# A decoder layer on one core: y's first two quads turned once for both token blocks, and diff queries and keys copied two units earlier

## The chip, the core and the metric

The kernel runs on one core of a Trainium2 chip. The metric is the device time of one execution in microseconds (us). The engines are named as in the profile: PE is TensorE (PEld its weight loads), DVE is VectorE, ACT is ScalarE, POOL is GpSimd and SP is SyncE. SP and POOL issue the transfers (DMA). Each engine takes its instructions in the order in which they stand in its queue, and an instruction that waits holds back all those behind it.

## The reference

One decoder layer in float32 for 256 tokens of width 2048: a half-step SwiGLU feed-forward net, a token mixer, a second feed-forward net, each followed by a residual sum and a layer norm. The change lies in the mixer, which is, cut to what matters:

```python
c_q, c_kv, k_r, dq, dk, dv, gate_mla, gate_diff = _split_columns(h @ w_in)
o_mla  = _mla_attention(q, k, v_mla)            # 8 heads, from c_q, c_kv, k_r
o_diff = _diff_attention(dq, dk, dv, positions, lam)   # 4 heads, two maps each
y = jax.nn.sigmoid(gate_mla) * (o_mla @ w_br_mla) + jax.nn.sigmoid(gate_diff) * (o_diff @ w_br_diff)
return y @ w_out
```

Here `dq`, `dk` and `dv` are 256 x 1024 each, and `y` is 256 x 2048.

## The kernel before, in words

**Tiles and units.** The 256 tokens are two blocks of 128 (b = 0 and 1). A product takes activations with the contracted dimension on the partitions as PE's stationary operand and a strip of weights as the moving one, and leaves a bank of 128 tokens x 512 columns. To keep float32 accuracy every operand is split into a high and a low part (`split`, L153-L156: a cast on ACT, L154, and a subtraction on DVE, L155), and each product is done three times (`triple`, L208-L210). Weights come from memory as 512 KB tiles `raw` or `sraw` (through SP in the main), are split into a pair of tiles of the ring `wring`, and are used. One such tile is a *unit* of work: 12 products when it serves both token blocks, 6 in the products of the seven-product scheme (`Hybrid`).

**Order of the work.** The program is written as a stream of units (`unit`, `advance`): load, split, and some units later the products. After the products of every unit a clock `tick` runs; `later(n, fn)` puts a piece of work n ticks ahead. So the rest of the layer (turning, softmax, norms) is threaded between the products by due times counted in units. A planner then places each engine's instructions: it goes by this order among those whose data it reckons to be there, and may put a later one first. In the last part of the mixer (`project`) each unit's products for block 1 come after the next unit's products for block 0, so block 1 of a result is done one unit after block 0.

**Turning a result.** A result has tokens on the partitions; the next product needs its columns there. Some results are turned on PE (`rows_to_quad`, L668 on; the transpositions are L671). Others make a trip through memory: `turn_out` (L711-L718) turns 32 x 32 blocks on DVE (`blocks`, L715) and writes them with four transfers on POOL (L717, 64 KB each) to a `turn` tensor in memory, arranged so that a plain read gives the whole turned; `turn` (L723-L731) reads it back `wait` units later with one POOL transfer into a tile `turned` (L729, 256 KB), and hands it to its user `more` units after that. The user is either a put into an activation quad (a quad is 512 columns, split by L154 and L155) or an ACT copy (L737, `turn_to_cols`) into a tile of columns.

**Where it happens.** `pair_cols` makes the turned diff queries and keys, `dqT` and `dkT`, four trips each (two halves, two blocks), with the copy 10 units after the read. `branch_diff` and `branch_mla` make y in four quads f = 0..3: first the four `branch_diff` results (4 units each), then the four `branch_mla` results (4 units each), and in its `done` (L1374-L1376 on DVE) the sum with the two gates; the sum lies in the tile that the profile calls `diff`. Quads 0 and 1 of y go through memory, quads 2 and 3 over PE. The product with `w_out` follows at once and takes the quads in order, two units a quad; its first products need quad 0. The layer norm after it, created just before, fetches rows through SP into tiles of the tag "tmp".

**Slots.** Tiles share slots by tag: "tmp" has 6 slots of 128 x 512 (the trips' `blocks` and `turned`, results before turning, rows for the norm), "act" has 41 of 128 x 1024. A tile waits for a slot until an earlier one's last reader is done.

Of the kernel before, what the change touches and what calls it, by code (L numbers as in the profile page):

```python
# [11 lines left out]
F32 = mybir.dt.float32  # L12
# [6 lines left out]
P = 128  # L19
# [40 lines left out]
def layer_kernel(ctx: ExitStack, tc: tile.TileContext, a: dict, out: bass.AP):  # L60
    nc = tc.nc
    V, S, GP, PE = nc.vector, nc.scalar, nc.gpsimd, nc.tensor
# [9 lines left out]
    def nm(s):  # L72
        uid[0] += 1
        return f"{s}_{uid[0]}"

    def act_tile(shape, dt=F32, name="act"):
        return apool.tile(shape, dt, tag="act", name=nm(name), bufs=SLOTS)

    def tmp_tile(shape, name="tmp", dt=F32):
        return small.tile(shape, dt, tag="tmp", name=nm(name), bufs=6)  # L80
# [22 lines left out]
    def later(n, fn):  # L103
        uid[0] += 1
        heapq.heappush(todo, (step[0] + n, uid[0], fn))
# [562 lines left out]
    def rows_to_quad(src, b, x, q, gain=None, shift=None, shared=False):  # L668
        t = tr_bank()
        for i in range(4):  # L670
            PE.transpose(t[:, i * P:(i + 1) * P], src[:, i * P:(i + 1) * P], ident)  # L671
        if gain is not None:
            full = x.raw(q, b) if q in x.kept else tmp_tile([P, 512], "full")
            if shared and q % 2 == 1:
                v, o = (u.rearrange("p (i t) -> p i t", i=4) for u in (full, t))
                g, b0 = (u[:, 4 * q:4 * q + 4].unsqueeze(2).to_broadcast([P, 4, P]) for u in (gain, shift))
                with tc.issue_after(x.made[q - 3, b].ins) if q > 2 else nullcontext():
                    V.tensor_tensor(out=v, in0=o, in1=g, op=ALU.mult)
                V.tensor_tensor(out=v, in0=v, in1=b0, op=ALU.add)
            else:  # L680
                for i in range(4):
                    k = 4 * q + i
                    S.activation(full[:, i * P:(i + 1) * P], t[:, i * P:(i + 1) * P], AF.Identity,
                                 bias=shift[:, k:k + 1], scale=gain[:, k:k + 1])
            t = full
        x.put(q, b, t.rearrange("p (i t) -> p i t", i=4))
# [25 lines left out]
    def turn_out(row, to):  # L712

        t = tmp_tile([P, 512], "blocks")
        V.transpose(t, row)  # L715
        for i in range(4):
            nc.gpsimd.dma_start(to.rearrange("(g r) (i f) -> i r g f", g=4, i=4)[i],  # L717
                                t[32 * i:32 * (i + 1), :].rearrange("r (g f) -> r g f", g=4))  # L718

    def turned(v):  # L720
        return v.rearrange("p (i k c) -> p k i c", i=4, k=4)

    def turn(row, use, wait, more):  # L723
        to = dram.tile([P, 512], F32, name=nm("turn"))
        turn_out(row, to)

        def back():
            t = tmp_tile([P, 512], "turned")
            nc.gpsimd.dma_start(t, to)  # L729
            later(more, lambda: use(turned(t)))  # L730
        later(wait, back)  # L731

    def turn_to_quad(row, b, x, q, wait, more):
        turn(row, lambda t: x.put(q, b, t), wait, more)

    def turn_to_cols(row, dst, b, wait, more):
        turn(row, lambda t: S.copy(dst[:, :, b * P:(b + 1) * P].rearrange("p k (i c) -> p k i c", i=4), t), wait, more)  # L737
# [393 lines left out]
    def mixer(x):  # L1131
# [58 lines left out]
        def whole(t, bank, snap, op):  # L1190
            if snap is None:
                S.copy(t, bank)
            else:
                V.tensor_tensor(out=t, in0=bank, in1=snap, op=op)
# [13 lines left out]
        def pair_cols(w, name):  # L1208
            dst = [act_tile([P, 4, T], F32, name) for _ in range(2)]

            def done(n, b, bank, snap, op):
                t = tmp_tile([P, 512], name + "r")
                whole(t, bank, snap, op)
                later(1, lambda: turn_to_cols(t, dst[n], b, 4, 10))
            hy.group(w[0], w[1], done, False, True)
            return dst

# [4 lines left out]
        back = {}  # L1222
# [137 lines left out]
        yq = Acts(KD, "y")  # L1360
# [6 lines left out]
        def branch_mla(f):  # L1367
            g0, g1 = gates.pop(f)
            y = diff_rows.pop(f)
            for t in (g0, g1):  # L1370
                S.activation(t, t, AF.Sigmoid)

            def done(b, bank):
                V.tensor_tensor(out=y[:, b, :], in0=y[:, b, :], in1=g1[:, b, :], op=ALU.mult)  # L1374
                V.tensor_tensor(out=g0[:, b, :], in0=bank, in1=g0[:, b, :], op=ALU.mult)
                V.tensor_tensor(out=y[:, b, :], in0=y[:, b, :], in1=g0[:, b, :], op=ALU.add)  # L1376
                if f < 2:
                    later(1, lambda: turn_to_quad(y[:, b, :], b, yq, f, 4, 6))
                else:
                    later(2, lambda: rows_to_quad(y[:, b, :], b, yq, f))  # L1380
            project(a["wbm"][f], om, MH, 512, done)
# [12 lines left out]
    dram = ctx.enter_context(tc.tile_pool(name="dram", bufs=1, space=bass.MemoryType.DRAM))  # L1394
# [27 lines left out]
    yq = mixer(h1)  # L1422
# [97 lines left out]
```

## Time and profile before

| | |
|---|---|
| median of 3 runs | 1967.31 us (1966.36 to 1968.93) |
| the profiled execution | 1969.03 us, span of its trace 1967.3 us |
| PE, share of the span busy | 1951.7 us, 99% |
| DVE / ACT / POOL | 1777.8 us, 90% / 1249.7 us, 64% / 309.3 us, 16% |
| granted TensorE clock | 0.998 |
| moved by DMA | 488.83 MB, 248 GB/s in the mean |

The profile is that of one execution, whose own time stands above. A matmul starts before the one ahead of it has ended, and the ends are modelled, so PE's share says that it is rarely empty, not that it runs at its peak. In the rows below, a timeline row is: start and length in us, engine, line and operation, what is written from what, sizes, how many were merged, and in brackets how long the engine stood idle before it and what ended that. A row of the chain is: start, length, and what the end of the execution hung on there.

### The profile page before, as it was taken

The numbers are of one execution on the slowest core, as the hardware profiler recorded it, in microseconds if no ns is written. First come the engines' busy times: TensorE is split into PE (matmuls) and PEld (weight loads), VectorE is DVE, ScalarE is ACT, GpSimd is POOL, SyncE is SP. The second block draws the span as 40 slices with busy tenths as digits, with TensorE's granted clock in tenths as the row PEclk, the third lists the DMA queues.
The fourth block names the chain that finished last, engine by engine and source line by source line (L and its number), as shares of the span: only waits on it lengthen the run. The fifth ranks groups of instructions, "written<-read, shape, count | busy, mean of one in ns | idle before, by whom it ended". The sixth has DMA issues, their size and how long they took to land.

```text
span 1967.3 us, 25772 instructions
## 1 busy us (share of the span) xinstructions
PE 1951.7 (99%) x8760; PEld 1618.2 (82%) x8760; DVE 1777.8 (90%) x2183; ACT 1249.7 (64%) x1634; POOL 309.3 (16%) x531
## 2 busy tenths in 40 slices
PE   9999999999999999999999999999999999999997
PEld 8888888888888898888888887888888888888886
DVE  7999999998998879988987676789999999999986
ACT  6666766676655666666667654556676666765661
POOL 0112111122100010102241530001211112210000
PEclk9999999999999999999999999999999999999999
DMA  8978888878776666767685788678888878787773
GB/s 315 285 227 262 268 261 247 259 234 306 271 238 214 208 223 248 246 223 262 203 248 196 236 295 274 198 261 255 255 267 264 250 238 271 251 314 236 277 233 121
DMA packets 149779, 488.83 MB, mean 248 GB/s; under 512 B 21600, under 2 KB 21648, under 8 KB 149648
## 3 DMA queue, kind: packets, MB, share of 16 engines
q1 hardware_dynamic: 119088, 401.13, 59.5%
q0 software_dynamic: 30560, 86.07, 16.8%
q8 instruction: 68, 1.11, 0.2%
q14 instruction: 63, 0.52, 0.1%
HBM read 456.71 MB, written 30.41 MB: 248 GB/s over the span
## 4 chain that ended last, share of the span: by engine, by line
PE 92%; DMA 3%; DVE 1%; issue 1%; ACT 1%; POOL 1%; SPq 0%; DVEq 0%; POOLq 0%; ACTq 0%
PE mm L209 29%; PE mm L208 29%; PE mm L210 29%; DMA turned<-turn 1%; DMA gate<-gates 1%; PE tr L210 1%; PE tr L209 1%; PE tr L208 1%; DMA turn<-blocks 0%; POOL turn L717 0%; PE tr L671 0%; ACT wring L154 0%; DMA raw<-in_wgd_dram 0%; DMA raw<-in_gu_dram 0%; PE tr L1322 0%
## 5 line engine op out<-in xcount | busy, mean ns | idle before, releaser
L154 ACT CAST wring<-raw 128x1024 fp32r<-128x1024 f32 (+2 forms) x467 | 481.9, 1037 | 322.3 <-PE mm L210 236.7
L155 DVE TENSOR_TENSOR wring<-raw,wring 128x1024 fp32r<-128x1024 f32 (+2 forms) x467 | 557.4, 1201 | 91.7 <-ACT wring L154 89.4
L154 ACT CAST wring<-sraw 128x1024 fp32r<-128x1024 f32 x436 | 453.0, 1052 | 201.9 <-DVE sraw L428 85.7
L155 DVE TENSOR_TENSOR wring<-sraw,wring 128x1024 fp32r<-128x1024 f32 x436 | 520.7, 1219 | 23.6 <-ACT wring L154 20.7
L208 PE MATMUL mm<-wring,h 128*128 128x512 f32 (+2 forms) x1248 | 480.9, 385 | 0.0
L210 PE MATMUL mm<-wring,h 128*128 128x512 f32 (+2 forms) x1248 | 480.3, 385 | 0.0
L209 PE MATMUL mm<-wring,h 128*128 128x512 f32 (+2 forms) x1248 | 480.0, 385 | 0.0
L208 PE MATMUL mm<-wring,xs 128*128 128x512 f32 x776 | 302.2, 389 | 0.6 <-ACT snap L385 0.6
L209 PE MATMUL mm<-wring,xs 128*128 128x512 f32 x776 | 301.9, 389 | 0.0
L210 PE MATMUL mm<-wring,xs 128*128 128x512 f32 x776 | 301.9, 389 | 0.0
L208 PEld LDWEIGHTS mm<-wring,h 128*128 128x128 f32 x1248 | 234.5, 188 | 46.9 <-ACT h L154 0.6
L209 PEld LDWEIGHTS mm<-wring,h 128*128 128x128 f32 x1248 | 234.5, 188 | 46.5 <-DVE wring L155 0.4
L210 PEld LDWEIGHTS mm<-wring,h 128*128 128x128 f32 x1248 | 234.4, 188 | 46.5 <-DVE h L155 0.7
L428 DVE TENSOR_TENSOR sraw<-sraw,sraw 128x1024 f32<-128x1024 f32 x168 | 199.2, 1219 | 2.0 <-DMA sraw<-in_wgm_dram 1.2
L208 PEld LDWEIGHTS mm<-wring,xs 128*128 128x128 f32 x776 | 145.7, 188 | 31.2 <-ACT snap L385 1.0
L210 PEld LDWEIGHTS mm<-wring,xs 128*128 128x128 f32 x776 | 145.7, 188 | 30.2
L209 PEld LDWEIGHTS mm<-wring,xs 128*128 128x128 f32 x776 | 145.7, 188 | 30.1
L717 POOL DMA_DIRECT2D hT<-blocks x176 | 96.8, 562 | 367.0 <-DVE blocks L715 366.0
L209 PE MATMUL mm<-wring,x 128*128 128x512 f32 x336 | 130.8, 389 | 0.5 <-DVE wring L155 0.5
L208 PE MATMUL mm<-wring,x 128*128 128x512 f32 x336 | 130.8, 390 | 0.0
L210 PE MATMUL mm<-wring,x 128*128 128x512 f32 x336 | 130.6, 389 | 0.0
L430 POOL DMA_DIRECT2D sraw<-in_gu_dram x40 | 35.5, 889 | 371.3 <-DVE sraw L428 288.3
(310 smaller groups left out, 2286.7 us busy)
## 6 DMA issues: line engine op xcount, KB each, us to landing
sraw<-in_gu_dram SPq DMA_DIRECT2D x160, 512.0 KB, 5.2
raw<-in_gu_dram SPq DMA_DIRECT2D x159, 512.0 KB, 4.9
raw<-in_dn_dram SPq DMA_DIRECT2D x140, 512.0 KB, 4.7
sraw<-in_gu_dram POOLq DMA_DIRECT2D x40, 512.0 KB, 7.1
sraw<-in_dn_dram SPq DMA_DIRECT2D x36, 512.0 KB, 5.2
eraw<-in_gu_dram SPq DMA_DIRECT2D x64, 256.0 KB, 5.8
raw<-in_w_out_dram SPq DMA_DIRECT2D x32, 512.0 KB, 4.3
hraw<-hT POOLq DMA_DIRECT2D x56, 256.0 KB, 5.8
```

The lines of the kernel that those rows point to most:

```text
L154: cast[0] = S.copy(hi, src)
L155: lows[0] = V.tensor_tensor(out=lo, in0=src, in1=hi.bitcast(F32), op=ALU.subtract)
L208: PE.matmul(o, xh, wh, start=first, stop=False, skip_group_check=again)
L209: PE.matmul(o, xh, wl, start=False, stop=False, skip_group_check=again)
L210: PE.matmul(o, xl, wh, start=False, stop=last, skip_group_check=again)
L428: last = V.tensor_tensor(out=R[src][i], in0=R[src][i], in1=R[add[1]][i], op=ALU.add)
L430: nc.gpsimd.dma_start(R["12"][s], source("22", s), accum_op=ALU.add)
L717: nc.gpsimd.dma_start(to.rearrange("(g r) (i f) -> i r g f", g=4, i=4)[i], t[32 * i:32 * (i + 1), :].rearrange("r (g f) -> r g f", g=4))
```

## The change

The first part adds `turn_both`, which makes one trip for both token blocks of a quad: one transposition of 128 x 1024, four writes of 128 KB, one read of 512 KB, and then the two uses, one unit apart. `branch_mla` calls it for quads 0 and 1 when block 1 is done, with 3 units to the read and 5 (block 0) and 6 (block 1) units to the use; before, each block went by itself, with 4 and 6. Its tiles `blocks` and `turned` are of the tag "act" instead of "tmp". The second part changes one number in `pair_cols`: the copy of a turned `dq` or `dk` tile is due 8 units after its read, not 10.

```diff
-    def turn_to_quad(row, b, x, q, wait, more):
-        turn(row, lambda t: x.put(q, b, t), wait, more)
+    def turn_both(rows, use, wait, more):
+
+        t = act_tile([P, 2, 512], F32, "blocks")
+        V.transpose(t.rearrange("p b f -> p (b f)"), rows.rearrange("p b f -> p (b f)"))
+        to = dram.tile([P, 2, 512], F32, name=nm("turn"))
+        for i in range(4):
+            nc.gpsimd.dma_start(to.rearrange("(g r) b (i f) -> i r b g f", g=4, i=4)[i],
+                                t[32 * i:32 * (i + 1)].rearrange("r b (g f) -> r b g f", g=4))
+
+        def back():
+            t = act_tile([P, 2, 512], F32, "turned")
+            nc.gpsimd.dma_start(t, to)
+            for b in range(2):
+                later(more + b, lambda b=b: use(b, turned(t[:, b, :])))
+        later(wait, back)
...
-                later(1, lambda: turn_to_cols(t, dst[n], b, 4, 10))
+                later(1, lambda: turn_to_cols(t, dst[n], b, 4, 8))
...
                 if f < 2:
-                    later(1, lambda: turn_to_quad(y[:, b, :], b, yq, f, 4, 6))
+                    if b == 1:
+                        later(1, lambda: turn_both(y, lambda n, t: yq.put(f, n, t), 3, 5))
                 else:
                     later(2, lambda: rows_to_quad(y[:, b, :], b, yq, f))
```

## The prediction

> **What bounds the kernel now.** I read the page first (busy time, then the chain's shares by engine), then the waits of TensorE alone (who waited for whom, us in total, times, longest), then the busy times by stretch, then the chain and the timelines around the two places that the diff touches.
>
> ```profile
> PE 1951.7 (99%) x8760; PEld 1618.2 (82%) x8760; DVE 1777.8 (90%) x2183; ACT 1249.7 (64%) x1634; POOL 309.3 (16%) x531
> ...
> PE 92%; DMA 3%; DVE 1%; issue 1%; ACT 1%; POOL 1%; SPq 0%; DVEq 0%; POOLq 0%; ACTq 0%
> ```
>
> ```profile
> PE tr L671 <- DVE diff L1376: 1.8, 1, 1.8
> ...
> PE mm L208 <- ACT snap L385: 0.6, 1, 0.6
> ```
>
> ```profile
> 1200.00:1956.00 756.00, 755.89 (x3348) 624.86 (x3347) 695.74 (x803) 468.77 (x586) 94.69 (x156) 1.00 0.77 248
> ```
>
> TensorE (PE) is busy 99% of the span and carries 92% of the chain. The change removes no product, so it can win only what PE waits. That is little: the largest wait (L671 on L1376) lies in the stage where y is turned, the second (L208 on L385) beside the turns of the diff keys. From 1200 to 1956, behind both, PE idles 0.11 us in all: what is won before stays won.
>
> ```profile
> 1184.80 0.39 PE L208 MATMUL mm<-wring,om 128*128 128x512 f32 x1
> 1185.03 0.39 PE L209 MATMUL mm<-wring,om 128*128 128x512 f32 x1
> 1185.25 0.39 PE L210 MATMUL mm<-wring,om 128*128 128x512 f32 x1
> 1187.49 0.63 PE L671 MATMUL tr<-ident,diff 128*128 128x128 f32 x4 [1.84 <-DVE diff L1376]
> ```
>
> Products start every 0.23 us. From 1185.25 to 1187.49 are 2.24 us, so the hole is worth 2.24 - 0.23 = 2.01 us, and the transposition on PE would have been due at 1185.48. The chain says what was late:
>
> ```profile
> 1159.35 5.02 DMA turn<-blocks
> ...
> 1164.90 5.83 DMA turned<-turn
> ...
> 1171.01 4.25 DMA turn<-blocks
> ...
> 1175.38 1.26 issue
> 1176.64 6.99 DMA turned<-turn
> ...
> 1183.66 0.63 ACT y L154
> ...
> 1184.31 0.04 DVE y L155
> ...
> 1184.92 0.68 DVE gate L1375
> ```
>
> Four trips (two quads, two token blocks) run one after the other through the POOL queue. The last comes back at 1176.64 + 6.99 = 1183.63; only then do ACT's cast and DVE's subtraction of that block run, and the gate product of the last quad (L1375, L1376), which PE's transposition needs, stands behind them on DVE. From landing to PE's start: 1187.49 - 1183.63 = 3.86 us.
>
> **The change, part one: y's quads 0 and 1.** Per quad it removes two trips (2 transpositions on DVE, 8 writes, 2 reads, all on POOL) and adds one (1 transposition of 128x1024, 4 writes, 1 read). The trip begins at the second block, one unit after the first, reads back 3 units later instead of 4, and puts the two blocks 5 and 6 units after that: every put stands one unit sooner.
>
> ```profile
> L715 DVE STREAM_TRANSPOSE blocks<-diff 128x512 f32<-128x512 f32 x4 | 2.8, 706 | 0.0
> L1119 DVE STREAM_TRANSPOSE pblocks<-p 128x384 f32<-128x384 f32 x3 | 1.7, 579 | 0.1
> ```
>
> ```profile
> 1156.72 0.70 DVE L715 STREAM_TRANSPOSE blocks<-diff 128x512 f32<-128x512 f32 x1
> ...
> 1163.70 0.69 DVE L1376 TENSOR_TENSOR diff<-diff,gate 128x512 f32<-128x512 f32 x1
> ...
> 1165.44 0.70 DVE L715 STREAM_TRANSPOSE blocks<-diff 128x512 f32<-128x512 f32 x1
> ```
>
> ```profile
> 1157.72 2.17 POOL L717 DMA_DIRECT2D turn<-blocks  x4 [0.87 <-DVE blocks L715]
> 1159.89 0.56 POOL L729 DMA_DIRECT2D turned<-turn  x1
> 1164.90 0.55 POOL L729 DMA_DIRECT2D turned<-turn  x1 [4.46 <-DMA turn<-blocks]
> 1165.45 3.82 POOL L717 DMA_DIRECT2D turn<-blocks  x7
> 1171.01 0.55 POOL L717 DMA_DIRECT2D turn<-blocks  x1 [1.75 <-DMA turned<-turn]
> ```
>
> ```profile
> sraw<-in_gu_dram POOLq DMA_DIRECT2D x40, 512.0 KB, 7.1
> ...
> turned<-turn POOLq DMA_DIRECT2D x26, 256.0 KB, 4.3
> ```
>
> DVE: 128 more elements cost 706 - 579 = 127 ns, so 1024 take 706 + 4 x 127 = 1214 ns (an estimate) against 2 x 706; 0.2 us saved per quad, hidden. POOL: four issues take 2.17 us; if twice the bytes cost nothing more in issuing, a quad's trip needs 2.17 + 0.55 us instead of twice that. Two stalls of POOL go: the 4.46 us in which the read of quad 0's second block held back quad 1's writes, and the 1.75 us in which quad 1's last write waited for a read to land (with five transfers a quad instead of ten I expect it to find a free place).
>
> Quad 0, first: the transposition stands where that of its second block does today, 1156.72, and ends 1.21 later at 1157.9. With 0.3 us to POOL, the fourth write is issued at 1158.2 + 3 x 0.55 = 1159.85, lands 5.02 later at 1164.9, and the read is issued at 1165.4. For the double read I take 7.1 us, the row of the same size on the same queue, since the 256 KB reads lie between 2.9 and 7.0; it lands at 1172.5. Today's first cast stands at 1175.29; one unit of 2.7 us (12 products of 0.23) sooner it would find the data there:
>
> ```profile
> DMA to landing us min/median/max: 2.9/4.3/7.0
> ```
>
> ```profile
> 1175.29 0.62 ACT L154 CAST y<-turned 128x512 fp32r<-128x512 f32 x1
> ...
> 1183.66 0.62 ACT L154 CAST y<-turned 128x512 fp32r<-128x512 f32 x1 [4.55 <-DMA turned<-turn]
> ```
>
> Quad 1, which decides: its last sum ends at 1163.70 + 0.69 = 1164.39; the transposition starts at 1165.44 as before and ends at 1166.65. POOL is free (read of quad 0 out by 1166), the fourth write is issued at 1166.95 + 3 x 0.55 = 1168.6, lands 4.25 to 5.02 later (1172.85 to 1173.6), and the read goes out 0.5 to 1.3 us after that, at 1173.4 to 1174.9 instead of 1176.64. With 7.1 us it lands at 1180.5 to 1182.0; I take the middle, 1181.3. Now both blocks come at once: two casts and two subtractions stand before L1375, one block more than today. On DVE that is 0.61 us more (1184.92 - 1184.31, the pitch today), so PE starts at landing + 3.86 + 0.61 = landing + 4.47. PE is on time (1185.48) if the landing is at 1181.0 or before. At 1181.3 a hole of 0.3 us is left: 2.0 - 0.3 = 1.7 us won. Bounds: landing by 1176.3 (a 2.9 us read from 1173.4) wins the whole 2.0; two reads of 6.99 one after the other from 1174.9 land at 1188.9 and cost 1188.9 - 1183.0 = 5.9 us. The break-even landing is 1183.0 and 0.2% (3.9 us) is lost from 1187.0 on. Queue and size point to 7.1, so I stay near the lower end.
>
> The Trainium skill (DMA: Bandwidth & Descriptors, section Anatomy of one DMA) gives a POOL transfer about 2 us plus its bytes over 436 GB/s: 3.2 us for 512 KB as an estimate, 2.6 for 256 KB. By that rule the landing would be at 1177.4 and nothing of the hole left (2.0 won). The trace doesn't agree here: 256 KB took 4.3 us in the median and 6.99 in this place, among the weights, so my sum goes by the row.
>
> The new tiles come from the 41-slot tag instead of the six slots of "tmp"; ring, y, branch inputs, gates and rows count about 28 there by the code, so I price a wait for a slot at nothing; if that cover is gone, it delays one transposition. The freed "tmp" slots let the gain and bias rows for the next norm be fetched sooner on SP, ahead of weights: their bytes are in the upper bound above.
>
> **Part two: the copies of turned dq and dk.** Only the place of eight ACT copies (0.61 us each) moves, two units sooner; no transfer, nothing on SP or POOL moves with them, and the reads stay where they are.
>
> ```profile
> 957.67 0.39 PE L210 MATMUL mm<-wring,h 128*128 128x512 f32 x1
> 958.66 0.50 PE L208 MATMUL mm<-wring,xs 128*128 128x512 f32 x1 [0.61 <-ACT snap L385]
> ```
>
> ```profile
> 953.86 0.59 ACT L386 COPY snap<-mm 128x512 f32<-128x512 f32 x1 [0.85 <-DVE dkTr L1194]
> ...
> 955.30 0.61 ACT L737 COPY dkT<-turned 128x512 f32<-128x512 f32 x1
> 956.13 2.00 ACT L154 CAST wring<-sraw 128x1024 fp32r<-128x1024 f32 x2 [0.22 <-DVE sraw L428]
> 958.03 0.58 ACT L385 COPY snap<-mm 128x512 f32<-128x512 f32 x1
> ...
> 965.09 1.05 ACT L154 CAST wring<-sraw 128x1024 fp32r<-128x1024 f32 x1 [2.75 <-DMA sraw<-in_wdv_dram]
> ...
> 969.99 0.62 ACT L737 COPY dkT<-turned 128x512 f32<-128x512 f32 x1 [2.38 <-DMA turned<-turn]
> ```
>
> The first dk copy stands just ahead of the snapshot that PE waits for (958.66 - 957.67 - 0.23 = 0.76 us). Two units up it can fall into the 0.85 us that ACT idles before 953.86, and frees its "tmp" slot for the next turns. The casts between still wait for DVE (0.22), so the whole 0.76 won't go: I take 0.3, bounds 0 and 0.76. Against it: the third dk copy already waits 2.38 us for its read; ahead of the cast at 965.09 it would hold ACT until 969.99 with two casts behind it, 2 x 1.05 us late. By the code four units are prepared ahead of PE there, so I take 0; its bound is 2.1 us lost. The dq copies wait for nothing today and PE has no hole there: 0.
>
> **The sum.** 1.7 + 0.3 = 2.0 us. The profiled execution took 1969.03 us (span 1967.3 and 1.7 around it); with the change 1967.0. The median of the runs, 1967.31, is 1.7 below the profiled one, so the forecast is 1965.3.
>
> **The rivals.** *The same wait at the same time*: the double read lands between 1182.4 and 1183.6, or another instruction takes the hole's place; 1966.7 to 1968 us. For it: one read must bring what two brought, and a 256 KB read in this place took 6.99. Against it: it leaves 2 to 3 us sooner.
>
> *Slower by queueing*: quad 1's writes, issued from 1166.95, go out behind quad 0's double read on POOL's queue and only move when it has landed. Today's rows show something of it: the write at 1171.01 follows a read and takes 4.25. Then the writes land at 1172.5 + 4.25 = 1176.8, the read leaves at 1177.5 and lands at 1184.6: PE's hole is 1184.6 + 4.47 - 1185.48 = 3.6 us, 1.6 more than now, so 1968.9 us; with the 1.26 us of issue and a read slower by 1.6 us it passes 1187.0 and 1971.2. Against it: the read of 1164.90 shared the queue with seven writes behind it and took 5.83. The Trainium skill (same page, section Queues, rings and completion order) says that one queue's descriptors on a DMA engine are taken in ring order, which is this rival; the trace so far bears it out only in that one row, so I give it its chance and not the forecast.
>
> *ACT held by a dk copy*: the 2.1 us above beside what part one wins: 1967.3 - 1.7 + 2.1 = 1967.7; were two more copies held so, 4.2 us more, 1971.9. Against it: ACT waits for PE in most places, and the planner puts a copy where it reckons its data to be.
>
> **How the numbers follow.** Forecast 0.55 (own range 1963.6 to 1966.7), the same wait 0.17, queueing 0.20 (half of it above 1971.2), ACT held 0.08 (half). About 0.2% is what a measurement of this kernel can tell from no change, 1963.4 to 1971.2 here. Faster by more needs both holes gone and more besides (2.0 + 0.76 = 2.8 us): 0.06, out of the forecast. Slower by more: 0.10 + 0.04 = 0.14. Within: 0.80. The range runs from 1963.3 (all of 2.8 and the 0.95 us by which the lowest run lay under the median) to 1971.3 (where queueing begins to count).
>
> **What the changed profile would show.** The wait of L671 on L1376 near 1185 shrinks from 1.84 to under 0.5; the last y cast from a turned tile stands near 1181.3 and waits less than 4.55; POOL's read of quad 1 goes out at 1173.4 to 1174.9; no write of a turn waits for a read; the DVE transposition takes 1.2 us. A first dk copy ahead of 953.86, and a wait on L385 under 0.6, would show part two right. The prediction is wrong if the double read needs over 9 us, if quad 1's writes land after 1176, or if the order on ACT and DVE shifts elsewhere so that PE's other stages, full today, open.

## The result, and the profile after

The changed kernel takes 1972.44 us in the median of 10 runs (1970.64 to 1974.90), the kernel before 1967.76 us in the median of 10 (1966.36 to 1969.34). The ratio is 1.0025, with a 95% interval of 1.0016 to 1.0034: slower by 4.7 us, by a little more than a measurement of this kernel can tell, and outside the predicted range.

The profiled execution of the changed kernel took 1973.44 us, its span 1971.7 us, 4.4 more than the profiled one of before. First the page's busy line and chain shares, then the waits of TensorE (who waited for whom: us in total, times, longest us):

```profile
PE 1953.6 (99%) x8760; PEld 1618.8 (82%) x8760; DVE 1778.3 (90%) x2181; ACT 1249.8 (63%) x1634; POOL 304.7 (15%) x521
...
PE 96%; DMA 2%; DVE 1%; issue 1%; ACT 0%; POOL 0%; SPq 0%; DVEq 0%; ACTq 0%; POOLq 0%
```

```profile
PE tr L671 <- DVE diff L1389: 3.7, 1, 3.7
PE mm L209 <- DVE wring L155: 1.2, 2, 0.7
```

The wait that the change was predicted to shrink (L671, now on L1389, from 1.8 us) has doubled. TensorE's timeline around it:

```profile
1186.10 0.39 PE L210 MATMUL mm<-wring,om 128*128 128x512 f32 x1
1190.21 1.09 PE L671 MATMUL tr<-ident,diff 128*128 128x128 f32 x4 [3.72 <-DVE diff L1389]
1190.95 0.78 PE L208 MATMUL mm<-wring,y 128*128 128x512 f32 x1
1191.52 0.63 PE L209 MATMUL mm<-wring,y 128*128 128x512 f32 x1
...
1193.64 0.40 PE L208 MATMUL mm<-wring,y 128*128 128x512 f32 x1
```

From 1186.10 to 1190.21 are 4.11 us; less the 0.23 of a product, the hole is worth 3.88, where it was worth 2.01. And something new follows it: a product takes 0.63 us in place of 0.39, for 3.43 us (1190.21 to 1193.64). The busy times by stretch (us, then PE, PEld, DVE, ACT, POOL with counts, granted clock, DMA share, GB/s) show the cause in the clock column:

```profile
1189.00:1190.00 1.00, 0.00 (x0) 0.00 (x0) 0.96 (x3) 0.37 (x1) 0.00 (x0) 1.00 0.21 49
1190.00:1191.00 1.00, 0.79 (x5) 0.82 (x5) 1.00 (x2) 0.00 (x0) 0.00 (x0) 0.60 0.95 340
1191.00:1192.00 1.00, 1.00 (x5) 0.81 (x4) 0.96 (x3) 0.59 (x1) 0.00 (x0) 0.50 0.34 135
1192.00:1193.00 1.00, 1.00 (x4) 0.81 (x3) 1.00 (x2) 0.00 (x0) 0.00 (x0) 0.50 0.77 176
1193.00:1194.00 1.00, 1.00 (x5) 0.77 (x4) 1.00 (x2) 0.00 (x0) 0.00 (x0) 0.70 0.88 344
```

The granted clock fell to half. The four transpositions and six products from 1190.21 to 1193.64 took 3.43 us; in the kernel before the same ten, from 1187.49, took 1.85. The product that follows these ten there is

```profile
1189.34 0.40 PE L208 MATMUL mm<-wring,y 128*128 128x512 f32 x1
```

The clock cost 1.58 us. With the hole's growth (1.87) that makes 3.45 of the 4.4 us; the rest is a difference of early waits between the two executions (the 1.2 us of the second wait row, 0.5 before; the new 0.7 stands at 946.7, and neither e3 nor e6 below shows it) and some 0.3 us spread out.

Why the hole is there is told by the chain, that is, by what each step waited for, from quad 1's transposition to the sum that PE needed:

```profile
1166.29 1.25 DVE blocks L736
1167.54 0.28 issue
1167.82 1.84 POOL turn L739 x3
1169.67 7.29 DMA turn<-blocks
...
1177.62 7.74 DMA turned<-turn
...
1185.39 0.05 ACT y L154
...
1186.53 0.95 ACT wring L154
...
1187.51 1.22 DVE wring L155
1188.73 0.61 DVE gate L1388
...
1189.37 0.70 DVE diff L1389
```

Quad 1's read leaves at 1177.62 (before: its second block's at 1176.64), lands at 1185.37 (before: 1183.63), and TensorE goes on 4.84 us after that, at 1190.21 (before: 3.86). Between the landing and the sum stands a cast of weights on ScalarE.

### The profile page after: what moved, and what is told of

It is laid out like the page before. It is cut to its first block, busy times and chain, and to the rows that moved or that the text cites. A ratio compares the mean times of both kernels' runs of the same rounds, so it can differ in the third digit from the quotient of the medians.

```text
span 1971.7 us, 25750 instructions
## 1 busy us (share of the span) xinstructions
PE 1953.6 (99%) x8760; PEld 1618.8 (82%) x8760; DVE 1778.3 (90%) x2181; ACT 1249.8 (63%) x1634; POOL 304.7 (15%) x521
## 4 chain that ended last, share of the span: by engine, by line
PE 96%; DMA 2%; DVE 1%; issue 1%; ACT 0%; POOL 0%; SPq 0%; DVEq 0%; ACTq 0%; POOLq 0%
PE mm L209 30%; PE mm L208 30%; PE mm L210 30%; PE tr L208 1%; PE tr L209 1%; PE tr L210 1%; DMA turned<-turn 1%; PE tr L671 0%; DVE wring L155 0%; DMA turn<-blocks 0%; DMA sraw<-in_wdv_dram 0%; ACT wring L154 0%; DMA raw<-in_gu_dram 0%; PE tr L1335 0%; PE tr L1263 0%
```

## The experiments

In the diffs, "-" is the kernel that is named ahead of each. No experiment leaves out or changes a part of the computation, save that e5 adds products whose outcome is overwritten.

**e1 and e2: is it the order on VectorE?** The subtractions of quad 1 wait for the late read, and the sums of quad 3 stand behind them. The edit puts them behind, in the changed kernel (e1) and in the one before (e2).

```diff
+        sums = [None]
+
+        def put_behind(f, b, t):
+            with tc.issue_after(sums[0].ins) if f == 1 else nullcontext():
+                yq.put(f, b, t)
...
-                V.tensor_tensor(out=y[:, b, :], in0=y[:, b, :], in1=g0[:, b, :], op=ALU.add)
+                sums[0] = V.tensor_tensor(out=y[:, b, :], in0=y[:, b, :], in1=g0[:, b, :], op=ALU.add)
...
-                        later(1, lambda: turn_both(y, lambda n, t: yq.put(f, n, t), 3, 5))
+                        later(1, lambda: turn_both(y, lambda n, t: put_behind(f, n, t), 3, 5))
```

> The changed kernel, with one order written out: the casts' subtractions of quad 1 of y (y<-turned) are issued on VectorE behind the latest sum of diff (L1389). The trip stays as late as it is (read landing at 1185.4). Main theory: the 4.1 us hole of TensorE at 1186.1 is there because those subtractions, which wait for the late read, stand ahead of the quad-3 sum in VectorE's queue; moved behind it, the hole goes and with it the 3.4 us at half the granted clock: about 1972.4 - 3.9 - 1.7 = 1966.8, and no clock under 1.00 between 1185 and 1200. A rival, by which the product itself needs quad 1 of y at that point and the late landing is the whole of it: 1971 or more, the hole moved from the transposition (L671) to the product behind it (L208).

> The kernel before, with the same order written out as in e1. Main theory: the hole of 2.23 us there (1185.25 to 1187.49) is the same queue on VectorE, and goes: 1967.8 - 2.0 = 1965.8. If the hole were the chain of the gate itself (product, sigmoid, sum), nothing changes: 1967.8.

Measured: e1 1972.99 us (ratio to before 1.0025, 1.0015 to 1.0035), no better than the changed kernel. e2 1967.25 us against 1967.89 of the kernel before (0.9997, 0.9988 to 1.0006), its profile without a hole there, but the time not measurably changed. In e1 VectorE's subtractions did move behind, and its timeline, with one row of ScalarE's ahead, names the queue that holds:

```profile
1184.43 1.14 ACT L154 CAST y<-turned 128x512 fp32r<-128x512 f32 x2 [5.38 <-DMA turned<-turn]
1185.48 2.93 ACT L154 CAST wring<-raw 128x1024 fp32r<-128x1024 f32 x3
```

```profile
1186.55 1.23 DVE L155 TENSOR_TENSOR wring<-raw,wring 128x1024 fp32r<-128x1024 f32 x1 [6.12 <-ACT wring L154]
1187.69 0.68 DVE L1394 TENSOR_TENSOR gate<-mm,gate 128x512 f32<-128x512 f32 x1
1188.41 0.69 DVE L1395 TENSOR_TENSOR diff<-diff,gate 128x512 f32<-128x512 f32 x1
```

ScalarE waited 5.38 us for the read with the casts of y at its head, and three casts of weights stood behind. VectorE, now free of y, waited 6.12 us for the first of those, because its subtraction of that weight tile stands ahead of the sum. The theory had the mechanism (a queue held by an instruction that waits for the read) and the wrong queue. The hole was still 1189.25 - 1185.72 - 0.23 = 3.30 us.

**e9, e10, e11: is it ScalarE's queue?** In e9 the cast of quad 1's turned blocks is made on VectorE, behind the sums like the subtraction, so that nothing on ScalarE waits for the read. e10 is the same in the kernel before; e11 is e9 with e3's edit (below). Against e1:

```diff
+    on_v = [False]
+
     def split(hi, lo, src):
-        cast[0] = S.copy(hi, src)
+        cast[0] = V.tensor_copy(out=hi, in_=src) if on_v[0] else S.copy(hi, src)
...
             with tc.issue_after(sums[0].ins) if f == 1 else nullcontext():
+                on_v[0] = f == 1
                 yq.put(f, b, t)
+                on_v[0] = False
```

> The changed kernel; the cast of quad 1's turned blocks (y<-turned) is made on VectorE instead of ScalarE, and both halves of it are issued there behind the latest sum of diff (L1389). Nothing on ScalarE then waits for quad 1's read. New theory, after e1 left the hole: what the late read holds is ScalarE's queue, where the casts of the weights that the sums' own queue waits for stand behind y<-turned. Then the hole of 4.1 us goes with its half clock, though the read lands no sooner: 1972.4 - 3.9 - 1.7 = 1966.8, some 0.5 more for two casts added to VectorE. If the late read holds the product itself, a hole of 2 us or more shows in front of a product (L208) and the time stays over 1970.

> The kernel before with e9's edit. New theory: no hole in front of quad 3's transposition in any run, where the profiled run of before had one of 2.2 us and that of e6 none; 1966.3 to 1967.3 by the 1967.25 that e2 measured, and less spread. If before has no hole in most of its runs, nothing to measure: 1967.5 to 1968.

> e9 with the first gain and bias rows asked for two units later, as in e3. With ScalarE free, the landing of the read should not matter any more: the same as e9 within 0.5 us. If the rows themselves cost something (e3 came out 2 us above before though its hole was only 0.6 us longer), it is above e9 by 1 us or more.

Measured: e9 1967.96 us (0.9998, 0.9989 to 1.0007), e10 1967.63 (0.9998, 0.9989 to 1.0007), e11 1968.51 (0.9999, 0.9990 to 1.0008), all against 1968.22 of the kernel before. So the step from e1 to e9, which moves only the casts, is worth 5 us, the whole loss; and none of the three beats the kernel before. e11 lies 0.55 us above e9, which can't be told from nothing: with ScalarE free, the rows that e3 and e11 move cost nothing measurable. In e9's profiled execution the read landed at 1181.6, sooner than in e1's (1184.41), so the profile that shows the mechanism is e11's, beside e3's, which has ScalarE's casts. Their reads are alike: out at 1174.65 and landed after 8.2 us in e11, out at 1174.90 and landed after 8.39 in e3. TensorE in e11, then in e3:

```profile
1185.24 0.40 PE L212 MATMUL mm<-wring,om 128*128 128x512 f32 x1
1185.47 0.60 PE L673 MATMUL tr<-ident,diff 128*128 128x128 f32 x4
```

```profile
1185.31 0.39 PE L210 MATMUL mm<-wring,om 128*128 128x512 f32 x1
1188.14 0.63 PE L671 MATMUL tr<-ident,diff 128*128 128x128 f32 x4 [2.45 <-DVE diff L1389]
```

With nearly the same landing (1182.85 and 1183.30) there is no hole when ScalarE is free, and one of 2.60 us when it is not. In e11 ScalarE's cast of weights stands behind a wait for TensorE, not for the read, and the sum is done 1.0 us after the landing:

```profile
1182.94 1.05 ACT L156 CAST wring<-raw 128x1024 fp32r<-128x1024 f32 x1 [1.67 <-PE mm L212]
```

```profile
1183.17 0.69 DVE L1399 TENSOR_TENSOR diff<-diff,gate 128x512 f32<-128x512 f32 x1
```

The products themselves don't need quad 1 of y at that time: in e9 VectorE subtracts its second block only at 1189.18, and TensorE's stretch from 1185 to 1190 is full.

**e3: what made the trip late?** In the changed kernel the first gain and bias rows (`gp`) of the norm are issued on SP at 1167.03 and 1167.52, after two loads of `w_out`; before, the first stood at 1175.44, after four. e3 makes them due two units later and leaves their use where it was (the first two lines of the edit also bring the same use in another norm two units forward). Against the changed kernel:

```diff
-                later(4, lambda: use(0))
-                later(6, lambda: use(1))
+                later(4 - 2 * (c == 0), lambda: use(0))
+                later(6 - 2 * (c == 0), lambda: use(1))
...
-                   (a["ln1_g"], a["ln1_b"]), (2, 7, 14, 21), lambda: yq.made[3, 1])
+                   (a["ln1_g"], a["ln1_b"]), (4, 7, 14, 21), lambda: yq.made[3, 1])
```

> The changed kernel, but the first rows of gain and bias of the next norm (gp) are asked for two units later, behind the fourth w_out load, where the kernel before has them. Main theory (quad 1's four writes were held from 1170.3 to 1176.9 by transfers pulled ahead of them): the writes land near 1173, the read leaves near 1174.5 and lands near 1182, the hole shrinks to at most 0.5 us and the clock stays at 1.00: 1966 to 1968. Rivals, by which the joint trip is this late by itself (its size, its later start) or by the full queues of weights that are there either way: the writes still land after 1176, the hole stays at 3 us or more, 1971.5 to 1973.

Measured: 1969.80 us (1.0011, 1.0003 to 1.0020). Its chain at the place:

```profile
1168.88 5.36 DMA turn<-blocks
...
1174.90 8.39 DMA turned<-turn
...
1188.01 0.14 issue
```

The last write takes 5.36 us in place of 7.29, and the read leaves at 1174.90, as expected. This holds over the profiles: where the rows go early, POOL stands idle between the fourth write and the read for 7.34 us (changed kernel), 7.48 (e1), 7.58 (e5), 7.48 (e8) and 7.02 (e9); where they go late, 5.41 (e3) and 5.24 (e11). But the read then took 8.39 us, so it landed at 1183.30, later than the 1182 that I expected, and a hole of 2.60 us stayed. So the rows cost some 2 us of lateness (how they hold the writes back, by their bytes or otherwise, is not shown), and what is left of the loss, 1.9 us, comes without them.

**e4, e7, e8: which part of the change?** e4 is the kernel before with only the tag of the trips' tiles changed. e7 and e8 are the changed kernel with only quad 0, or only quad 1, in a joint trip.

```diff
-        t = tmp_tile([P, 512], "blocks")
+        t = (tile or tmp_tile)([P, 512], name="blocks")
...
-                    later(1, lambda: turn_to_quad(y[:, b, :], b, yq, f, 4, 6))
+                    later(1, lambda: turn(y[:, b, :], lambda t: yq.put(f, b, t), 4, 6, act_tile))
```

```diff
-                    if b == 1:
-                        later(1, lambda: turn_both(y, lambda n, t: yq.put(f, n, t), 3, 5))
+                    if f == 0:
+                        if b == 1:
+                            later(1, lambda: turn_both(y, lambda n, t: yq.put(f, n, t), 3, 5))
+                    else:
+                        later(1, lambda: turn(y[:, b, :], lambda t: yq.put(f, b, t), 4, 6))
```

> The kernel before, each block of y still turned in a trip of its own, but the tiles blocks and turned taken from the 41 slots (act) as in the change. The gates' last pair, the cols and the gp rows are then issued at about the places they have in the changed kernel. Rival of the tag (what moved is what costs): a hole of 3.5 us or more and 1971 to 1973. Main theory: the gp rows are ahead here too, so it should lose some, but the single trips start earlier, so less: 1967.8 to 1970. The rival of the joint trip by itself: 1967.8.

> The changed kernel, with only quad 0 of y turned in one joint trip; quad 1's blocks go one by one as before. The first gp rows are issued ahead of later w_out loads here too. Main theory: four writes of quad 1 stand behind quad 0's read as before, and some are held by the transfers ahead: a hole of 2 to 4 us, 1967.5 to 1972. If quad 1's joint trip is what loses: 1967.8 or less.

> The changed kernel, with only quad 1 of y turned in one joint trip; quad 0's blocks go one by one as before. The gp rows are ahead of the w_out loads as in the changed kernel. Main theory and the rival of the joint trip by itself: quad 1's writes are as late as in the changed kernel, hole 3.5 us or more, 1971 to 1973. If the reordering of the gates by quad 0's joint trip is what loses: 1967.8.

Measured: e4 1968.24 us (1.0000, 0.9991 to 1.0009), e7 1967.76 (1.0000, 0.9992 to 1.0009), e8 1970.47 (1.0014, 1.0006 to 1.0023). The tag alone and quad 0's joint trip cost nothing that can be measured; with quad 1's joint trip 2.5 us are lost. e8's rows went early too (1167.55, behind two loads), so its 2.5 us may hold both. But early rows are in e4 as well (1170.45, behind two loads), with single trips and no measurable loss, and e3 has the joint trips without early rows and loses 1.9: the joint trip of quad 1 is what costs, and by e3 the rows add to it. For e7 my premise was wrong: its rows went out at 1176.19, behind five loads, so it says nothing of early rows. In e8 the read left at 1178.28, as late as expected, but took only 5.07 us, and the hole was 2.07 us instead of the 3.5 that I had written.

**e5: the clock.** Products of zeros are put into the hole of the changed kernel, ahead of the transposition that overwrites their bank.

```diff
-                    later(2, lambda: rows_to_quad(y[:, b, :], b, yq, f))
+                    later(2, lambda: rows_to_quad(y[:, b, :], b, yq, f, fill=16 if (f, b) == (3, 0) else 0))
...
+        if fill:
+            with tc.issue_after(last_mm[0].ins):
+                for i in range(fill):
+                    PE.matmul(t[:, 0:P], zero, zero, start=True, stop=True)
```

> The changed kernel, with 16 matmuls of a tile of zeros, 128x128, put on TensorE behind the last product before the transposition of quad 3, block 0, into the bank that the transposition then overwrites; at the 0.1 us that one 128x128 transposition takes there they fill some 1.6 to 2 us of the hole. The transposition still waits for VectorE until about 1190.2. If the fall of the granted clock to 0.50 comes of TensorE standing idle for more than some 3 us, the clock stays at 1.00 and the time is 1972.4 - 1.7 = 1970.7. If the fall has another cause, it stays, and the time with it: 1972.4.

Measured: 1971.27 us (1.0019, 1.0010 to 1.0028), 1.2 under the changed kernel. TensorE at the place, and the stretch behind it:

```profile
1185.76 3.73 PE L675 MATMUL tr<-zero 128*128 128x128 f32 x32
1189.63 0.66 PE L677 MATMUL tr<-ident,diff 128*128 128x128 f32 x4
```

```profile
1190.00:1195.00 5.00, 5.00 (x27) 4.14 (x26) 4.58 (x6) 2.12 (x3) 0.00 (x0) 1.00 0.68 215
```

The sixteen appear as 32 and took 3.73 us, twice what I had reckoned, and filled the hole whole; the transposition still came when VectorE's sum was there. The clock stayed at 1.00. So the fall comes of TensorE's idleness. The price of 1.58 us is read from the timeline; the medians, 1.2 us apart, fit it but do not show it by themselves, since the two intervals overlap (1.0010 to 1.0028 here, 1.0016 to 1.0034 for the changed kernel). Nor does a profile say in which of the changed kernel's executions the clock fell.

**e6: the copies alone.** The kernel before with only `turn_to_cols(t, dst[n], b, 4, 8)`.

> The second part of the change alone: copies of diff's turned queries and keys two units sooner, y turned as before. The instructions come out in the same order on every engine as in the kernel before, so this part does nothing: 1967.8 within 0.5, by every theory but one; the rival that the copies hold ScalarE says 1968.5 or more, the prediction's own term 1967.5.

Measured: 1967.03 us against 1968.01 (0.9998, 0.9989 to 1.0006). The copies' new due time changes no engine's order. So e6 is a second look at the order of the kernel before, and there the hole of 1185 is missing. VectorE at the place:

```profile
1182.69 0.69 DVE L155 TENSOR_TENSOR y<-turned,y 128x512 fp32r<-128x512 f32 x1 [0.70 <-ACT y L154]
1183.31 0.68 DVE L1388 TENSOR_TENSOR gate<-mm,gate 128x512 f32<-128x512 f32 x1
...
1185.04 0.68 DVE L1389 TENSOR_TENSOR diff<-diff,gate 128x512 f32<-128x512 f32 x1
```

The sum is ready at 1185.72, 1.6 us sooner than in the profiled execution of before (1186.65 + 0.69 = 1187.34): the last read left 0.45 us sooner and took 5.8 us instead of 6.99. TensorE also came 1.4 us later, at 1186.92 (it was due at 1185.48), having stood 0.8 us at another place (1137.96), so it didn't wait. By these two profiles, differences of this size between executions decide whether there is a hole at 1185.

**All runs together.** The hole in front of quad 3's transposition in each profile, the loss to the half clock behind it, and the median's excess over the kernel before (run beside it):

| run | hole us | clock us | excess us |
|---|---|---|---|
| kernel before | 2.01 | 0 | 0 |
| changed kernel | 3.88 | 1.58 | +4.7 |
| e1 | 3.30 | 1.57 | +5.1 |
| e5 | 3.87, filled | 0 | +3.3 |
| e3 | 2.60 | 0 | +1.9 |
| e8 | 2.07 | 0 | +2.5 |
| e4 | 0.86 | 0 | +0.4 |
| e2, e6, e7, e9, e10, e11 | 0 | 0 | -1.0 to +0.3 |

Hole and clock are of one execution, the excess is of medians. In the six rows below the first that have a hole, hole plus clock gives the excess to within 0.8 us; in the last row the difference can't be told from nothing. The kernel before stands apart: its profiled execution has a hole of 2.01 us and was itself 1.3 us above its median of ten.

## Why the prediction was wrong

- **The hole as what could be won.** It was read rightly (2.01 us, a trip's landing 3.86 us before PE), but it was taken for a part of every execution. The profiled one took 1969.03 us, 1.7 above the median of three that I had (1.3 above the later median of ten); I took 2.0 off for the change and then 1.7 off again for the step to the median. If the median run has no hole, that 1.7 largely *is* the hole, counted twice. e2 and e10, without a hole, are not measurably faster than the kernel before, and e6's profile of the same order has none. What the other runs of before looked like, no profile shows; by the medians of e2 and e10 (0.64 and 0.59 us under) there was about 0.6 us to win, which isn't told apart from nothing.
- **Part one, quad 1's read out at 1173.4 to 1174.9: the step that failed.** It left at 1177.62, 3.5 us behind the middle of that. The transposition stood 0.85 us later, but so did all the work there (TensorE's last product ahead of the hole at 1186.10, before at 1185.25), by the early waits of that execution, so this part added nothing to the hole; the other 2.6 us did. Four writes of 128 KB were issued at 0.62 us apart, not 0.55, 0.2 more; and the last write took 7.29 us where I had 4.25 to 5.02, 2.65 more, less 0.24 in the gap to the read. The rows that cause some 2 us of this are those that the prediction named ("ahead of weights: their bytes are in the upper bound above") and gave no term of their own.
- **The price of the late landing: the second step that failed.** Less the 0.85, the landing at 1185.37 lies 1.5 us behind the prediction's break-even of 1183.0. By its own rule that is 1968.8 us, slower but within its range. What took the time out of the range is what the rule lacked: 1.58 us at the half clock, 0.37 of a longer way from landing to TensorE (below), and a median of before in which the hole of 2.01 stands at most in part. From the median of ten, a kernel before without any hole would give 1967.76 + 3.88 + 1.58 = 1973.2, one with the whole hole 1971.2; 1972.44 lies between.
- **The double read of 7.1 us** took 7.74, and 5.1 to 8.4 in the experiments: right in size, with a wide spread. The Trainium skill's rule (DMA: Bandwidth & Descriptors, section Anatomy of one DMA), 3.2 us for this size as an estimate, does not agree: every read of quad 1 took over 5 us among the loads.
- **Landing plus 4.47** was 4.84, but by way of ScalarE: the prediction added only one more subtraction on VectorE, and left out the weight cast that stands behind both y casts on ScalarE. Its rule "slower from a landing at 1183.0 on" was about right.
- **The rival "slower by queueing"** had the course nearly to the digit (read out at 1177.5 against 1177.62, landing 1184.6 against 1185.37, hole 3.6 against 3.88) and gave 1968.9 us. Its cause was another: quad 0's double read, out at 1164.50, landed 4.8 us later, at 1169.3, while the last of quad 1's writes, issued at 1169.67, landed only at 1176.96; so it wasn't ring order on POOL's queue behind that read. That its numbers came so near is luck. And its price lacked the same things: the half clock, and what the median of before lacks of the hole.
- **Break-even and clock.** The price of a hole was taken to be its length. In e3 a hole of 2.60 us cost no more than that; behind those of 3.30 (e1) and 3.88 came 1.6 us at the half clock.
- **Slots** of the 41: e4 shows that taking them costs nothing measurable, as priced. That the freed "tmp" slots let `gp` go sooner was foreseen; its price wasn't.
- **Part two** was put at 0.3 us of gain. It moves no instruction (e6): the planner places the copies where it did before. The rival of ACT held by a dk copy falls for the same reason, though ScalarE held by a *y cast* was the mechanism.
- **"What is won before stays won"** held for what is lost as well: from 1200 to 1956 PE idled 0.12 us.

## What to carry to other kernels

A late transfer costs through the queue of the engine that consumes it, so ask what stands behind the consumer on *each* engine that touches the data: here two casts on ScalarE held the weights of the next units, and moving them to an engine where nothing urgent stood behind was worth 5 us with the transfer left as it was. Before pricing a hole seen in one profiled execution, compare that execution with the median: if it lies above by the size of the hole, the hole may not be there to win. And joining two transfers into one gives up the early half of the data: here it gained nothing measurable for quad 0 (e7) and lost time for quad 1 (e8).

## What the runs showed of the hardware

The granted clock of TensorE fell to 0.50 after holes of 4.11 us (changed kernel) and 3.53 us (e1, from 1185.72 to 1189.25), all from start to start, and stayed at 1.00 after holes of 2.83 (e3), 2.30 (e8) and 2.24 us (before), and when the hole was filled with zeros (e5). It stayed at 0.50 for about 3.4 us of work, from 1190.21 to 1193.64 in the changed kernel. In e1 the fall came only some 0.7 us after TensorE had taken up again, and the full clock 4.1 us after (1189.25 to 1193.36), by the pace of the products:

```profile
1188.00:1189.00 1.00, 0.00 (x0) 0.00 (x0) 0.96 (x2) 0.41 (x1) 0.00 (x0) 1.00 0.53 123
1189.00:1190.00 1.00, 0.75 (x6) 0.70 (x7) 1.00 (x2) 0.08 (x1) 0.00 (x0) 0.95 0.79 270
1190.00:1191.00 1.00, 1.00 (x4) 0.81 (x3) 0.96 (x3) 0.50 (x1) 0.00 (x0) 0.50 0.45 180
```

The Trainium skill (TensorE: Matmul & The Clock Gate, section Part 1: The HAM clock gate) states that the clock goes to half after an idle window of about 3.4 us and back after about as long of sustained work, with a window that runs free of the program. The 3.43 us, and a fall that comes at different distances from the hole, agree with it. The length of the idle window is not settled by these runs: in e1 TensorE's wait by the profile was 3.14 us, under 3.4, and the clock fell; in e3 it was 2.45, and it didn't.
